# Latent attention on one core: the value products of two key blocks issued as one group

## The chip, the cores and the metric

The kernel runs on one core of a Trainium2 chip. The metric is the time on the device of one execution, in microseconds. The engines are TensorE (PE in the profile; PEld is its loading of weights), VectorE (DVE), ScalarE (ACT), GpSimd (POOL) and SyncE (SP), which issues most of the DMAs.

## The reference

Two layers work on 1024 latent tokens and 256 context tokens of width 1024. Each layer has a mixer of three head groups (retention, latent attention, windowed attention), an output projection, and a mixture of 16 experts. The change touches the latent attention, whose core is, for each of 8 heads:

```python
s = (einsum('bhqr,bkr->bhqk', ql, kv) + einsum('bhqp,bkp->bhqk', qr, kr)) * scale
p = softmax(s, axis=-1)
ol = einsum('bhqk,bkr->bhqr', p, kv)
out = einsum('blhr,rhd->blhd', ol, w_uv)
```

Latent tokens attend to all 1280 keys (context and latent). Context tokens attend to the 256 context keys, and in the first layer only.

## The kernel before, in words

Each layer runs in this order: adaptive norm and input projection with retention and windowed attention beside it (`front`), latent attention (`mla`), output projection (`out_proj`), experts (`moe`). All of this is one program; a scheduler puts the instructions of each engine in an order of its own from their priorities and from when it expects their inputs, within the limits of the data and the buffers.

In `mla` the keys and queries of a head are made in split form (a high and a low part), and the products run transposed: keys on the partitions, queries along the columns. The 1280 keys are 10 blocks of 128 (`NB`), the 1024 latent queries two halves `u` of 512. `main` (line 1125) handles one head. For each key block `kb` and each half `u`:

- `scores` (line 1083) makes three matmuls of 512 columns into a PSUM bank `st`, of which there are three.
- ScalarE takes the exponential into `P[kb][:, u]` (line 1142). `P` has four buffers, each for one key block with both halves.
- GpSimd adds `P[kb]` to `acc` (lines 1146 and 1148), the column sums before they are reduced over the partitions.
- `values` (line 1131) makes the products of the block's values with P. The output of half `u` goes to partitions 64u to 64u+63 of the one bank `po`, so that one product takes 64 of the 128 columns of the array. Each of these float32 products shows as two matmul instructions. All blocks accumulate into `po`.

In the loop `values(kb - 1)` is called in the turn of block `kb`, and `values(NB - 1)` after the loop. Its products have top priority (`high_priority`), and their order among themselves on TensorE is fixed (`manual_schedule`). Between these steps `advance` takes steps of three generators that run beside: `prep(h + 1)`, which makes the keys and queries of the next head and their row maxima (`top`, line 971: a product into one of the banks `sm`, of which there are three, or `sx`, of which there is one, and a maximum by VectorE, line 974); `finish` of the head before (line 1090: the copy of `po`, the products of `acc` with a column of ones, the reciprocals, the scaling); and in layer 0 `context` (line 1110), the attention of the context tokens. The last head has no next one to prepare. Its call `before_last` opens what the output projection and the routing need.

The scheduler, and not the text of the loop, thus sets where a group of value products stands among the score and preparation products. The text gives it the groups, their order inside, and the block whose exponentials a group needs.

Of the kernel before, what the change touches and what calls it, by code (L numbers as in the profile page):

```python
# [23 lines left out]
NB = 10  # L24
# [90 lines left out]
def hybrid_kernel(tc, I, out, dbg=None):  # L115
# [4 lines left out]
    def T(pool, shape, dt, tag, bufs=None):  # L120
        cnt[0] += 1
        kw = {} if bufs is None else {"bufs": bufs}
        return pool.tile(list(shape), dt, tag=tag, name=f"{tag}_{cnt[0]}", **kw)

    def mm(o, a, b, start, stop):
        PE.matmul(o, a, b, start=start, stop=stop, skip_group_check=True)  # L126
# [135 lines left out]
    def advance(gen, n=1):  # L262
        for _ in range(n):
            if next(gen, "end") == "end":
                return False
        return True
# [675 lines left out]
    def mla(l, M, qp, mp):  # L942
# [140 lines left out]
        def scores(o, h, ks, qs):  # L1083
            qh, ql = qTs[h % 2]
            kh, kl = M["kTs"][h % 2]
            mm(o, kh[:, ks], qh[:, qs], True, False)
            mm(o, kh[0:96, ks], ql[:, qs], False, False)
            mm(o, kl[:, ks], qh[0:96, qs], False, True)

        def finish(h, po, acc, n, c0):  # L1090


            c = "" if n == 512 else "c"
            ys = T(rp, [128, n], F32, "ys" + c, 1)
            acopy(ys[:, 0:n], po[:, 0:n])
            yield
            ps = bank()
            for u in range(2):
                mm(ps[64 * u:64 * u + 64, 0:n], ones, acc[:, u, 0:n], True, True)
            rb = T(rp, [128, n], F32, "rb" + c, 1)  # L1100
            r0 = 64 * (h % 2)
            acopy(rb[:, 0:n], ps[:, 0:n])
            for a in range(0, n, 128):
                V.reciprocal(rb[:, a:a + 128], rb[:, a:a + 128])
                yield
            for u in range(2):
                V.tensor_tensor(yT[r0:r0 + 64, h // 2, c0 + u * n:c0 + (u + 1) * n], ys[64 * u:64 * u + 64, 0:n],
                                rb[64 * u:64 * u + 64, 0:n], OP.mult)

        def context(h):  # L1110
            st = T(pp, [128, 512], F32, "st", 3)
            for kb in range(2):
                scores(st[:, kb * 256:kb * 256 + 256], h, slice(kb * 128, kb * 128 + 128), slice(0, 256))
            pc = T(rp, [128, 2, 2, 128], F32, "pc", 1)
            S.activation(pc.rearrange("p k u t -> p (k u t)"), st, AF.Exp, scale=scale)
            acc = T(rp, [128, 2, 128], F32, "accc", 1)
            G.tensor_tensor(acc, pc[:, 0], pc[:, 1], OP.add)
            yield
            po = bank()
            for kb in range(2):  # L1120
                for u in range(2):
                    mm(po[64 * u:64 * u + 64, 0:128], M["vn"][:, kb, h * 64:(h + 1) * 64], pc[:, kb, u], kb == 0, kb == 1)
            yield from finish(h, po, acc, 128, 0)

        def main(h, nxt, prev):

            acc = T(rp, [128, 2, 512], F32, "acc")
            po = T(pp, [128, 512], F32, "po", 1)
            P = {}

            def values(kb):
                with tc.high_priority(), tc.manual_schedule(engines={mybir.EngineType.PE}):
                    for u in (1, 0):
                        mm(po[64 * u:64 * u + 64], M["vn"][:, kb, h * 64:(h + 1) * 64], P[kb][:, u], kb == 0, kb == NB - 1)

            cx = context(h) if qb0 == 0 else None
            for kb in range(NB):
                P[kb] = T(rp, [128, 2, 512], F32, "P", 4)
                for u in range(2):
                    st = T(pp, [128, 512], F32, "st", 3)  # L1140
                    scores(st, h, slice(kb * 128, kb * 128 + 128), slice(CTX + u * 512, CTX + u * 512 + 512))
                    S.activation(P[kb][:, u], st, AF.Exp, scale=scale)  # L1142
                    if nxt is not None:
                        advance(nxt)
                if kb == 1:
                    G.tensor_tensor(acc, P[0], P[1], OP.add)
                elif kb > 1:
                    G.tensor_tensor(acc, acc, P[kb], OP.add)  # L1148
                if nxt is not None:
                    advance(nxt)  # L1150
                if kb > 0:
                    values(kb - 1)
                if nxt is not None:
                    advance(nxt)
                if prev is not None and kb >= 5:
                    advance(prev)
                if cx is not None and kb >= 3:
                    advance(cx)
            values(NB - 1)
            end = finish(h, po, acc, 512, CTX)  # L1160
            advance(end)
            while nxt is not None and advance(nxt):
                pass
            return end

        def run(yT_, rp_, pp_, before_last):
            nonlocal yT, rp, pp
            yT, rp, pp = yT_, rp_, pp_

            for tag, shape, bufs in (("pc", [128, 2, 2, 128], 1), ("accc", [128, 2, 128], 1), ("P", [128, 2, 512], 4),  # L1170
                                     ("acc", [128, 2, 512], 2)):
                T(rp, shape, F32, tag, bufs)
            prev = None
            for h in range(8):
                if h == 7:
                    before_last()
                prev = main(h, prep(h + 1) if h < 7 else None, prev)
            while advance(prev):
                pass
# [800 lines left out]
```

## Time and profile before

| | us |
|---|---|
| median of 3 runs | 2990.1 |
| lowest and highest | 2983.69, 2990.77 |
| the profiled execution | 2985.17 |
| its span in the profile | 2983.0 |
| PE busy | 2750.1 (92%) |
| DVE busy | 2166.1 (73%) |
| ACT busy | 1574.6 (53%) |
| POOL busy | 698.7 (23%) |
| value products (`po<-P,vn`), PE busy | 183.8 in 640 matmuls |

Latent attention runs from about 490 to 812 us (layer 0) and from about 2050 to 2357 us (layer 1). In a timeline the first number is the start of a piece and the second its length. Matmuls are pipelined, so that one starts before the end shown of the one ahead; what each costs is read from start to start.

### The profile page before, as it was taken

To read this page: it belongs to the slowest core of one execution; us is meant where nothing else is said; L and a number is where in the kernel's file an instruction comes from. 1 tells how busy PE (TensorE), PEld (TensorE's weight loads), DVE (VectorE), ACT (ScalarE), POOL (GpSimd) and SP (SyncE) were. 2 spreads that over 40 slices of the span, in tenths; PEclk is the share of its full clock that TensorE was granted. 3 is DMA by queue.
4 is the path that set the end of the run, shared out by engine and by line. 5 is a ranking of instruction groups with operands and counts; after the bars stand their busy time and mean duration, and the time that the engine had idled before them with its cause. 6 is when DMAs were issued, how large, how long until landed. Compare 5 with 4: busy or idle time off the path is not lost. (4 is left out here: it accounts for less than half of the span.)

```text
span 2983.0 us, 41643 instructions
## 1 busy us (share of the span) xinstructions
PE 2750.1 (92%) x14702; PEld 1885.9 (63%) x14702; DVE 2166.1 (73%) x4688; ACT 1574.6 (53%) x2728; POOL 698.7 (23%) x561
## 2 busy tenths in 40 slices
PE   7999998999999799999998799998999995999996
PEld 3666775556466566666665666785555573777774
DVE  4455668788748777777775755567878578899997
ACT  3353545555533456665664544346555434777774
POOL 0011133555611111111111010133555521111110
PEclk8999998999999899999999899899999997999998
DMA  8621210000278578887886422210000247999995
GB/s 302 232 79 57 85 38 7 1 1 1 85 263 284 182 261 285 278 287 256 282 275 211 154 87 66 85 44 1 1 1 23 79 174 268 342 372 392 387 383 198
DMA packets 177740, 507.93 MB, mean 170 GB/s; under 512 B 27110, under 2 KB 38172, under 8 KB 172412
## 3 DMA queue, kind: packets, MB, share of 16 engines
q1 hardware_dynamic: 158796, 443.40, 41.5%
q0 software_dynamic: 13552, 43.00, 5.7%
q10 hardware_dynamic: 5184, 18.88, 1.6%
q8 instruction: 116, 1.90, 0.3%
q14 instruction: 92, 0.75, 0.1%
HBM read 448.74 MB, written 56.46 MB: 169 GB/s over the span
## 5 line engine op out<-in xcount | busy, mean ns | idle before, releaser
L136 DVE TENSOR_TENSOR wlo<-raw,whi 128x1536 fp32r<-128x1536 f32 (+3 forms) x496 | 688.9, 1406 | 148.0 <-ACT whi L130 144.9
L130 ACT ACTIVATE whi<-raw 128x1536 fp32r<-128x1536 f32 (+3 forms) x496 | 591.1, 1207 | 271.4 <-DMA raw<-in_exp_w_up_dram 89.9
L1148 POOL TENSOR_TENSOR acc<-acc,P 128x1024 f32<-128x1024 f32 x128 | 306.8, 2397 | 180.7 <-ACT P L1142 178.6
L126 PE MATMUL pp<-whi,hhs 128*128 128x512 f32 (+3 forms) x640 | 255.1, 400 | 4.4 <-DVE st L288 2.7
L1142 ACT ACTIVATE P<-st 128x512 f32<-128x512 f32 x320 | 187.3, 594 | 119.5 <-PE st L126 115.4
L126 PE MATMUL pp<-wlo,hhs 128*128 128x512 f32 (+3 forms) x640 | 248.6, 389 | 0.2 <-DVE wlo L136 0.2
L126 PE MATMUL pp<-whi,hl 128*128 128x512 f32 (+3 forms) x640 | 247.4, 387 | 0.8 <-DVE hl L136 0.7
L126 PE MATMUL pg<-whi,xh 128*128 128x512 f32 x720 | 224.7, 419 | 1.8 <-ACT xh L130 1.8
L126 PE MATMUL pg<-wlo,xh 128*128 128x512 f32 x720 | 213.3, 401 | 0.4 <-DVE wlo L136 0.3
L126 PE MATMUL pg<-whi,xl 128*128 128x512 f32 x720 | 210.0, 397 | 0.0
L1813 POOL DMA_INDIRECT xres<-ys,idx x31 | 82.4, 2658 | 523.0 <-DVE ys L1812 523.0
L974 DVE TENSOR_REDUCE mx<-sm 128x1 f32<-128x512 f32 (+1 forms) x308 | 172.2, 585 | 34.6 <-PE sm L126 31.1
L126 PE MATMUL po<-P,vn 128*64 128x512 f32 x640 | 183.8, 627 | 10.6 <-ACT P L1142 8.9
L126 PEld LDWEIGHTS pg<-whi,xh 128*128 128x128 f32 x720 | 128.9, 191 | 44.1 <-issue 19.8
L126 PEld LDWEIGHTS pg<-whi,xl 128*128 128x128 f32 x720 | 137.1, 191 | 29.5
L126 PEld LDWEIGHTS pg<-wlo,xh 128*128 128x128 f32 x720 | 136.0, 191 | 31.1 <-DVE wlo L136 1.8
L126 PEld LDWEIGHTS pp<-whi,hhs 128*128 128x128 f32 x640 | 125.1, 196 | 31.5 <-issue 5.1
L126 PEld LDWEIGHTS pp<-wlo,hhs 128*128 128x128 f32 x640 | 125.0, 195 | 24.4 <-issue 8.0
L126 PEld LDWEIGHTS pp<-whi,hl 128*128 128x128 f32 x640 | 125.2, 196 | 22.6 <-issue 3.8
L126 PE MATMUL st<-qTl,kTh 96*128 96x512 f32 (+1 forms) x336 | 137.7, 410 | 0.0
L126 PE MATMUL st<-qTh,kTh 97*128 97x512 f32 (+1 forms) x336 | 135.8, 404 | 1.9 <-ACT vn L130 1.3
L126 PE MATMUL st<-qTh,kTl 96*128 96x512 f32 (+1 forms) x336 | 132.8, 395 | 0.0
(502 smaller groups left out, 5581.5 us busy)
## 6 DMA issues: line engine op xcount, KB each, us to landing
raw<-in_exp_w_gate_dram SPq DMA_DIRECT2D x256, 384.0 KB
raw<-in_exp_w_up_dram SPq DMA_DIRECT2D x256, 384.0 KB
raw<-in_exp_w_down_dram SPq DMA_DIRECT2D x192, 512.0 KB
w<-in_ada_w_dram SPq DMA_DIRECT2D x40, 1024.0 KB
projd<-st SPq DMA_DIRECT2D x54, 256.0 KB
raw<-in_w_in_dram SPq DMA_DIRECT2D x48, 256.0 KB
hl<-in_ada_w_dram SPq DMA_DIRECT2D x16, 512.0 KB
xt<-in_x_dram SPq DMA_DIRECT2D x16, 512.0 KB
```

What stands on the lines that cost most here:

```text
L126: PE.matmul(o, a, b, start=start, stop=stop, skip_group_check=True)
L130: S.activation(o, i, AF.Copy)
L136: V.tensor_sub(lo, src, hi)
L974: V.tensor_reduce(mx[:, b, j:j + 1], o[:, 0:z - a], AX.X, OP.max)
L1142: S.activation(P[kb][:, u], st, AF.Exp, scale=scale)
L1148: G.tensor_tensor(acc, acc, P[kb], OP.add)
L1813: G.indirect_dma_start(out=xres[l], out_offset=bass.IndirectOffsetOnAxis(ap=idx[:, :1], axis=0), in_=ys, in_offset=None, compute_op=OP.add)
```

## The change

`values` makes the products of two key blocks, the newer one (`kb`) first and then the older (`kb - 1`), each with half 1 ahead of half 0. It is called in the turns of blocks 2, 4, 6 and 8, for the pairs (1, 0), (3, 2), (5, 4) and (7, 6), and after the loop for (9, 8). The accumulation therefore starts with block 1 and ends with block 8. Priority and the fixed order now cover the four products of a pair.

```diff
             def values(kb):
+
                 with tc.high_priority(), tc.manual_schedule(engines={mybir.EngineType.PE}):
-                    for u in (1, 0):
-                        mm(po[64 * u:64 * u + 64], M["vn"][:, kb, h * 64:(h + 1) * 64], P[kb][:, u], kb == 0, kb == NB - 1)
+                    for k in (kb, kb - 1):
+                        for u in (1, 0):
+                            mm(po[64 * u:64 * u + 64], M["vn"][:, k, h * 64:(h + 1) * 64], P[k][:, u], k == 1, k == NB - 2)
...
-                if kb > 0:
+                if kb > 0 and kb % 2 == 0:
                     values(kb - 1)
```

## Rows read from the trace of the kernel before

**Rows 1.** The page, busy time of each engine.

```profile
PE 2750.1 (92%) x14702; PEld 1885.9 (63%) x14702; DVE 2166.1 (73%) x4688; ACT 1574.6 (53%) x2728; POOL 698.7 (23%) x561
```

**Rows 2.** By stretch: length; PE, PEld, DVE, ACT, POOL busy; clock, DMA share, GB/s.

```profile
633.90:675.00 41.10, 39.85 (x182) 24.25 (x178) 35.07 (x62) 23.19 (x47) 22.02 (x11) 1.00 0.00 0
...
2112.00:2151.40 39.40, 37.81 (x159) 21.28 (x158) 31.56 (x57) 21.19 (x42) 21.47 (x9) 1.00 0.00 1
...
1200.00:1400.00 200.00, 193.09 (x1282) 131.83 (x1284) 154.00 (x169) 123.07 (x139) 34.66 (x18) 0.98 0.83 279
2540.00:2700.00 160.00, 160.00 (x751) 125.96 (x750) 151.02 (x165) 119.92 (x130) 20.40 (x11) 1.00 0.99 362
```

**Rows 3.** Timeline of TensorE, layer 0: one value group and its neighbours.

```profile
599.78 0.40 PE L126 MATMUL st<-qTl,kTh 96*128 96x512 f32 x1
600.11 1.08 PE L126 MATMUL po<-P,vn 128*64 128x512 f32 x4
601.12 0.49 PE L126 MATMUL st<-qTh,kTl 96*128 96x512 f32 x1
601.46 0.28 PE L126 MATMUL sx<-kTh,qTh 96*128 96x256 f32 x1
601.57 0.39 PE L126 MATMUL st<-qTh,kTh 97*128 97x512 f32 x1
...
602.04 0.40 PE L126 MATMUL st<-qTh,kTl 96*128 96x512 f32 x1
```

**Rows 4.** Value products of tile po; minimum, median, maximum in ns.

```profile
L126 PE MATMUL po<-P,vn x640: 592/593/1117, 490.8 to 2354.5; 128*64 128x512 f32 x160
```

**Rows 5.** Timeline of TensorE, start of the last head of layer 0.

```profile
781.39 2.06 PE L126 MATMUL po<-P,vn 128*64 128x512 f32 x8 [0.79 <-ACT ys L130]
783.37 0.50 PE L126 MATMUL st<-qTh,kTh 97*128 97x512 f32 x1
783.72 0.40 PE L126 MATMUL st<-qTl,kTh 96*128 96x512 f32 x1
```

**Rows 6.** Timeline of TensorE, layer 1, end of a head.

```profile
2108.13 0.64 PE L126 MATMUL po<-P,vn 128*64 128x512 f32 x1
2108.20 0.59 PE L126 MATMUL sm<-acc,mcst 128*64 128x512 f32 x1
```

**Rows 7.** Waits, layer 0, 590 to 757 us: total, times, longest.

```profile
PEld po L126 <- ACT P L1142: 12.7, 32, 0.7
...
PE po L126 <- ACT P L1142: 2.3, 8, 0.3
```

**Rows 8.** Waits, layer 1, 2110 to 2308 us.

```profile
PE po L126 <- ACT P L1142: 1.3, 3, 0.5
```

**Rows 9.** Waits, layer 0, 590 to 757 us, with VectorE in them.

```profile
DVE mx L974 <- PE sm L126: 7.5, 16, 1.2
...
DVE rb L1104 <- ACT rb L130: 4.8, 4, 1.2
DVE mx L974 <- PE sx L126: 4.8, 6, 1.2
...
DVE qTl L1019 <- ACT qTh L130: 4.6, 4, 1.1
...
PE sm L126 <- DVE mx L974: 2.4, 4, 0.6
```

**Rows 10.** By line, 592 to 757 us: busy, mean ns, idle before.

```profile
L1148 POOL TENSOR_TENSOR acc<-acc,P 128x1024 f32<-128x1024 f32 x33 | 78.3, 2372 | 47.3 <-ACT P L1142 47.3
...
L974 DVE TENSOR_REDUCE mx<-sm 128x1 f32<-128x512 f32 (+1 forms) x77 | 42.2, 575 | 7.2 <-PE sm L126 6.9
```

**Rows 11.** Timeline of TensorE, layer 1, the last head.

```profile
2346.39 1.08 PE L126 MATMUL po<-P,vn 128*64 128x512 f32 x4
...
2351.59 1.08 PE L126 MATMUL po<-P,vn 128*64 128x512 f32 x4
...
2356.68 1.98 PE L126 MATMUL sm<-acc,mcst 128*64 128x512 f32 x4 [1.58 <-POOL acc L1148]
```

## The prediction

> **What bounds the kernel now.** I read the page's busy shares first. TensorE is busy for 2750.1 of 2983.0 us, VectorE for 2166.1, ScalarE for 1574.6 [rows 1]. An average hides stages, so the second view is busy time by stretch. The change touches latent attention alone: eight heads in each of two layers. One head of layer 0 takes 41.1 us, in which TensorE is busy 39.85, VectorE 35.07, ScalarE 23.19, GpSimd 22.02 and DMA moves nothing; a head of layer 1 takes 39.4 us with TensorE at 37.81 [rows 2]. [...] The experts' stage that follows is again TensorE's (193.09 of 200 us, and 160.00 of 160 us in layer 1) [rows 2]. It starts when attention has ended, so what a head gives back should move everything behind it forward.
>
> The third view is the order of TensorE's instructions. Score products of 512 columns follow each other every 0.235 us (601.57 and, two on, 602.04) [rows 3]. The value products of one key block are four instructions of 64 columns, two at a time on the two halves of the array, together 1.01 us (600.11 to 601.12) [rows 3]. What the reader is to see is what stands around them: the matmul ahead has its successor 0.33 us after its start (599.78 to 600.11) where 0.235 is usual, and the first one behind needs 0.34 (601.12 to 601.46). About 0.1 us is thus lost on each side of a group.
>
> **What the change does, and the cost of each part.** Nothing is computed less: 640 value instructions stay, 4 for a block, so 160 blocks [rows 4]. The calls go from ten of one block to five of two blocks, for each head.
>
> *Merging two groups.* A group now costs 1.01 us and the two edges, 0.095 and 0.105: 1.21 us, two of them 2.42. The trace holds one place where two blocks ran back to back, at the start of the last head of layer 0: eight instructions from 781.39 to 783.37, 1.98 us, with 0.35 to the second score product behind [rows 5]. With the same edges that is 2.18 us. A merged pair saves 0.24 us. Two blocks of a head already share their edges with other 64-column work, for instance the block that runs among the products of the sums with a column of ones at 2108 us [rows 6]; I count those as saving nothing, and pair the other eight. 4 pairs x 16 heads x 0.24 = 15.4 us off the path. From below this term is 0 (pairs that do not form), from above 80 pairs x 0.24 = 19 us.
>
> [...]
>
> *Waiting for the exponentials.* A group at top priority is put on TensorE as soon as its exponentials are expected. TensorE's idle time for them is 2.3 us in 8 waits over four heads of layer 0 and 1.3 us in 3 waits over five heads of layer 1 [rows 7, 8], 0.58 and 0.26 us a head. With the newer block first a merged group waits once, for the later exponential, and the older block is long there. Half as many groups wait: 0.29 x 7 + 0.13 x 7 = 2.9 us gained. The weight-load rows put up to 12.7 us over four heads on the same releaser [rows 7], 3.2 us a head, but most of that is the 0.25 us edge already counted. From above, then, half of what is left, some 0.5 us a head, 7 us; from below, a loss: each of 64 groups may wait 0.2 us more, 13 us. I take 2.9, since that row is idle time of TensorE itself.
>
> *What stands behind a longer group.* For 2.0 instead of 1.0 us TensorE issues nothing else. Queued behind are score products, for which ScalarE waits, and products of the next head's preparation, for which VectorE waits. ScalarE has 18 us free in a head [rows 2] and three score banks. VectorE has 6.0 us free in layer 0; of these 7.5 + 4.8 us over four heads, 3.1 a head, are waits for TensorE's preparation banks [rows 9]. TensorE in turn waits 2.4 us over four heads, 0.6 a head, for VectorE to empty a bank [rows 9]. I let that grow by half, 0.3 us in each of the 14 heads that prepare another: 4.2 us lost. Bounds: 0, and the 20 us of the first rival.
>
> *Buffers of P.* The older block of a pair is held one block longer, with four buffers: two are held, two stay for blocks ahead. GpSimd's sum takes 2.37 us a block and was waiting for P before most of these [rows 10]. So it holds no buffer longer than TensorE does; cost nothing. If GpSimd did fall behind, the exponentials would come late next.
>
> *The end of a layer.* The last head has no preparation beside it. There a block takes 2.6 us (2346.39 and, two blocks on, 2351.59) and the last group is followed by a wait of 1.58 us for GpSimd's sum [rows 11]. GpSimd's 2.37 us is close to the 2.5 us that a block would take, and the last two sums come closer together. I take back half of the gain of both last heads: 1.0 us.
>
> *The single bank po.* The first products of a head need it free from the copy of the head before. Today they come with block 0, then with block 1, so the copy has more time: cost nothing.
>
> Sum: 15.4 + 2.9 - 4.2 - 1.0 = 13.1 us. The profiled execution took 2985.17 us (span 2983.0 and 2.2 around it); less 13.1 that is 2972. It lies 5 us below the median of the runs, 2990.1; the mean of these three and of the profiled one is 2987.4, from which the forecast is 2974.
>
> **The rivals.**
>
> 1. *Slower: VectorE starves during the long groups.* VectorE lives on what TensorE puts into four banks; a bank holds 0.58 us of its work on average [rows 10]. If its backlog at a group's start is 0.9 us, an old group of 1.2 us leaves it idle 0.3 us, ten times a head: 3 us, which is the 3.1 us seen. A merged one of 2.2 us leaves 1.3 us, five times: 6.5. With 35.1 us of work and 2.35 us of its other waits (4.8 + 4.6 over four heads [rows 9]) a head of layer 0 would then take 44.0 us, 2.9 more; over seven heads 20 us slower than 2987, about 3007. It decides if the backlog is below some 1.5 us, at which VectorE's total meets TensorE's new pace. Against it: all four banks full are 2.3 us, TensorE can fill a bank in 0.235 us, and preparation is due only at the head's end. [...] Chance 0.10.
>
> 2. *No change: the saved edges turn into waits.* The newer exponential is waited for with nothing of the older block left to run in the meantime. Today the older group could fill that time. At 0.2 us for each of 64 groups this is 12.8 us in place of the 2.9 gained; 15.4 - 12.8 - 4.2 - 1.0 is -2.6, so 2990. For it: waits of 0.3 us stand before present groups. Against it: score and preparation products fill today's gaps too. Chance 0.14.
>
> 3. *The change does not do what it says.* Order is fixed among the four products only; other matmuls may be put between the two blocks, as the column-of-ones products are today [rows 6]. If half the pairs are split, half of every term is left, 6.5 us: 2981. Chance 0.08.
>
> 4. *More than forecast.* If half of the upper wait bound comes too and VectorE costs nothing, 19 + 7 = 26 us, about 2961. Chance 0.08.
>
> **How the numbers follow.** The forecast has 0.60, and its own range is a gain of 9 to 20 us, 2967 to 2979. About 0.3% (9 us) is what a measurement of this kernel can tell from no change. Forecast and rival 4 lie beyond it: faster 0.68. Rivals 2 and 3 lie within it: same 0.22. Rival 1: slower 0.10. The range runs from rival 4, 2960, to 2991, past rivals 2 and 3 but short of the first, which leaves out some 0.15 to 0.2.
>
> **What would show it.** In the changed trace the value products should stand as runs of eight of about 1.98 us, some 64 to 80 of them, with an edge of 0.1 us at each end. Heads should take 40.3 and 38.6 us. TensorE's idle time for P should fall by about half. VectorE's waits for TensorE's banks may rise by 1 to 2 us a head without a longer head; if they rise and the head does not shorten, rival 1 is right. If TensorE's waits for P grow in place of the edges, it is rival 2; if runs of four remain, rival 3. The forecast is wrong if a head shortens by less than 0.5 us, or if a gain in the heads is lost again in the output projection or the experts.

## The result, and the profile after

The changed kernel takes 3029.3 us (median of 4 runs, 3027.0 to 3035.1) against 2989.3 us for the kernel before on the same chip: a ratio of 1.0136 with a 95% interval of 1.0118 to 1.0155. It is 40 us slower, where the sum had forecast 13 us less (2974). The profiled execution took 3030.5 us.

The page of the changed kernel, its busy times, to be held against [rows 1]:

```profile
span 3028.6 us, 41576 instructions
...
PE 2755.3 (91%) x14702; PEld 1904.1 (63%) x14702; DVE 2198.3 (73%) x4688; ACT 1571.3 (52%) x2728; POOL 703.4 (23%) x561
```

By this page every engine runs exactly as many instructions as before. TensorE's busy time has grown by 5 us only, though its groups are shorter. VectorE's has grown by 32 us with the same 4688 instructions, and that is the first thing to ask about.

The time is lost in latent attention. From the first value product to the last, layer 0 now takes 344.9 us instead of 317.0, layer 1 314.4 instead of 303.8: 38.5 of the 45.6 us by which the span grew. By stretch, two heads of layer 0, one of layer 1, and three stretches inside the first of them (columns as in [rows 2]):

```profile
610.22:657.67 47.45, 42.58 (x179) 25.88 (x178) 39.07 (x62) 22.89 (x48) 22.19 (x11) 0.93 0.00 1
657.67:705.37 47.70, 43.51 (x179) 26.90 (x178) 39.27 (x62) 22.92 (x48) 22.22 (x11) 0.89 0.00 0
2194.70:2236.70 42.00, 37.44 (x158) 22.56 (x157) 33.44 (x57) 20.66 (x42) 21.72 (x10) 0.96 0.00 1
610.22:632.00 21.78, 19.81 (x87) 11.76 (x86) 20.30 (x26) 11.19 (x23) 9.72 (x5) 1.00 0.00 0
632.00:639.20 7.20, 4.30 (x16) 2.63 (x15) 6.88 (x12) 4.12 (x9) 2.52 (x2) 0.90 0.00 0
639.20:643.20 4.00, 4.00 (x11) 0.94 (x10) 2.04 (x4) 0.14 (x1) 2.36 (x1) 0.50 0.00 0
```

The head of layer 0 shown in [rows 2] took 41.10 us, with 35.07 of VectorE in 62 instructions at a granted clock of 1.00. These take 47.5, with 39.1 us of VectorE in the same 62, and the clock is 0.93 and 0.89. Inside the first head it is 1.00 up to 632.0. In the next 7.2 us TensorE is busy for 4.3 only, while VectorE has hardly a gap, and the mean clock is 0.90: for the last 1.4 us of this stretch, from about 637.8 on, it is at 0.50, and it stays there in the stretch behind.

The groups themselves came out as meant. The value products of the changed kernel:

```profile
L126 PE MATMUL po<-P,vn x640: 592/592/1117, 492.2 to 2398.1; 128*64 128x512 f32 x160
```

They stand in 74 runs of eight; the other pairs, one in each of six heads, are split by products of the column sums. At a granted clock of 1.00 a run of eight takes 1.87 us to the start of its successor (627.94 to 629.81 in the timeline below). So what has to be explained is not the merged group.

### What VectorE does longer

Timelines of the changed kernel over the same 30 us of the first of these heads: VectorE, GpSimd, ScalarE and TensorE (start, length, instruction, idle time before it and what ended it). GpSimd's instructions here are its sums of P, the `acc` of line 1148 (the first of a head) and 1150.

```profile
618.42 3.52 DVE L1107 TENSOR_TENSOR yB<-ys,rb 64x512 f32<-64x512 f32 x2
...
628.08 2.79 DVE L1029 TENSOR_TENSOR qTl<-tb,qTh 32x512 fp32r<-32x512 f32 x1
...
632.34 0.68 DVE L1024 TENSOR_TENSOR tb<-tb,ta 32x512 f32<-32x512 f32 x1
...
633.96 0.68 DVE L1029 TENSOR_TENSOR qTl<-tb,qTh 32x512 fp32r<-32x512 f32 x1
...
636.03 1.82 DVE L1024 TENSOR_TENSOR tb<-tb,ta 32x256 f32<-32x256 f32 x1
```

```profile
615.88 4.82 POOL L1150 TENSOR_TENSOR acc<-acc,P 128x1024 f32<-128x1024 f32 x2 [2.96 <-ACT P L1144]
627.97 2.36 POOL L1148 TENSOR_TENSOR acc<-P,P 128x1024 f32<-128x1024 f32 x1 [7.27 <-ACT P L1144]
635.20 2.38 POOL L1150 TENSOR_TENSOR acc<-acc,P 128x1024 f32<-128x1024 f32 x1 [4.87 <-ACT P L1144]
```

```profile
621.98 0.60 ACT L130 ACTIVATE ys<-po 128x512 f32<-128x512 f32 x1 [1.05 <-DVE yB L1107]
...
633.06 0.63 ACT L130 ACTIVATE qTh<-tb 32x512 fp32r<-32x512 f32 x1 [2.33 <-DVE tb L1024]
633.71 0.60 ACT L1144 ACTIVATE P<-st 128x512 f32<-128x512 f32 x1
```

```profile
627.94 1.94 PE L126 MATMUL po<-P,vn 128*64 128x512 f32 x8 [0.88 <-ACT P L1144]
629.81 0.50 PE L126 MATMUL sm<-hhs,wqs 128*128 128x256 f32 x2
...
632.45 0.36 PE L126 MATMUL sx<-kTh,qTh 96*128 96x256 f32 x1 [0.38 <-DVE tb L1023]
...
634.36 0.50 PE L126 MATMUL st<-qTh,kTh 97*128 97x512 f32 x1 [0.74 <-ACT P L1144]
...
635.70 0.92 PE L126 MATMUL sm<-kTh,qTh 96*128 96x512 f32 x2 [0.60 <-DVE tb L1023]
...
638.36 0.79 PE L126 MATMUL sm<-kTh,qTh 96*128 96x512 f32 x1 [1.17 <-DVE mx L974]
...
639.51 3.68 PE L126 MATMUL po<-P,vn 128*64 128x512 f32 x8
643.12 0.80 PE L126 MATMUL sm<-kTh,qTh 96*128 96x512 f32 x1
```

Read it in order of time. The same instruction `qTl<-tb,qTh`, of the same shape, takes 0.68 us at 633.96 and 2.79 us at 628.08. At 628.08 GpSimd has just begun a sum, which ends at 630.33; the instruction ends at 630.87, 0.54 us later. What VectorE has behind it moves back by 2.1 us, among it `tb` at 632.34. ScalarE waits 2.33 us for that `tb`, and the exponential that stands behind it in ScalarE's order begins only at 633.71. TensorE runs out of score banks (0.74 us at 634.36). The next `tb`, at 636.03, meets the next sum: it takes 1.82 us, where the shortest of its shape takes 0.42, and ends 0.27 us after the sum. TensorE waits 1.17 us for the maximum that VectorE makes behind it (638.36). Within this wait its granted clock falls from 1.00 to 0.50, and a run of eight takes 3.61 us (639.51 to 643.12) instead of 1.87.

The pattern holds for four kinds of VectorE instruction whose two operands and output all lie in SBUF: `tb<-tb,ta` (line 1024 before and after), `qTl<-tb,qTh` (1029), and both forms of `yB` (1107), 132 in all. Reductions, reciprocals and operations with one operand in a PSUM bank keep their length beside GpSimd's sums. In the kernel before, beside a sum and without one, the maxima of 512 columns out of `sm` (line 974) take 673 to 693 and 664 to 693 ns, the reciprocals `rb<-rb` (1104) 891 to 953 and 894 to 954, and `tb<-sm,tabs` of 512 columns (1023), with one operand in a bank, 689 to 690 and 689. I call **excess** the sum, over these 132, of duration less the shortest of the same shape in the same run. It is 61.9 us before and 98.9 us after, in 50 and 61 instructions that are over 0.2 us too long. The tiles of the kernel before:

```profile
L1029 DVE TENSOR_TENSOR qTl<-tb,qTh x42: 417/550/1931, 493.9 to 2296.3; 32x512 fp32r<-32x512 f32 x21, 32x256 fp32r<-32x256 f32 x21
```

```profile
L1107 DVE TENSOR_TENSOR yB<-ys,rb x32: 683/944/2899, 568.2 to 2363.5; 64x512 f32<-64x512 f32 x32
```

and of the changed kernel:

```profile
L1029 DVE TENSOR_TENSOR qTl<-tb,qTh x42: 416/682/2794, 493.0 to 2344.6; 32x512 fp32r<-32x512 f32 x21, 32x256 fp32r<-32x256 f32 x21
```

```profile
L1107 DVE TENSOR_TENSOR yB<-ys,rb x32: 682/2232/2901, 571.2 to 2406.8; 64x512 f32<-64x512 f32 x32
```

Where no sum runs beside them, six `yB<-ys,rb` of the kernel before and ten of the changed one take 684 to 692 ns. This tile has one shape, and a maximum of four times the minimum was there to be read before the change already; after it even the median is three times the minimum. `qTl` has two shapes, whose shortest take 0.42 and 0.68 us; its maximum of 1.93 us before and 2.79 after lies far above both.

Who waits for these instructions stands in the waits of the whole run (total, times, longest). Before:

```profile
ACT qTh L130 <- DVE tb L1024: 35.3, 29, 2.8
...
PE sm L126 <- DVE mx L974: 9.3, 19, 0.6
PE po L126 <- ACT P L1142: 8.9, 19, 2.5
ACT ys L130 <- DVE yB L1107: 8.0, 7, 3.2
```

After:

```profile
ACT qTh L130 <- DVE tb L1024: 65.4, 33, 3.1
ACT ys L130 <- DVE yB L1107: 31.8, 13, 4.5
PE sm L126 <- DVE mx L974: 20.4, 23, 1.7
PE st L126 <- ACT qTh L130: 11.7, 6, 2.2
PE sm L126 <- DVE tb L1023: 8.1, 12, 1.7
PE po L126 <- ACT P L1144: 7.2, 12, 1.1
```

Two channels run from VectorE to TensorE. One is the query rotation of the next head: `tb` late, ScalarE's copy `qTh` late (35.3 to 65.4 us), and the exponentials behind it. The other is the end of the head before: `yB` reads the one buffer `ys`, ScalarE's copy of `po` into `ys` must wait for it (8.0 to 31.8 us), and again exponentials and `qTh` copies stand behind. TensorE's direct wait for P did not grow (8.9 to 7.2 us).

### The profile page after: what moved, and what is told of

Same layout as the page of the kernel before. It is cut to its first block, busy times and chain, and to the rows that moved or that the text cites. A ratio compares the mean times of both kernels' runs of the same rounds, so it can differ in the third digit from the quotient of the medians.

```text
span 3028.6 us, 41576 instructions
## 1 busy us (share of the span) xinstructions
PE 2755.3 (91%) x14702; PEld 1904.1 (63%) x14702; DVE 2198.3 (73%) x4688; ACT 1571.3 (52%) x2728; POOL 703.4 (23%) x561
## 5 line engine op out<-in xcount | busy, mean ns | idle before, releaser
L126 PE MATMUL po<-P,vn 128*64 128x512 f32 x640 | 174.4, 656 | 7.4 <-ACT P L1144 7.2
L126 PE MATMUL sm<-kTh,qTh 96*128 96x512 f32 (+1 forms) x308 | 113.1, 405 | 34.7 <-DVE mx L974 20.2
```

## The experiments

The theory, A in the texts on record: GpSimd's sum of P keeps VectorE's operations with both operands in SBUF standing; pairs shift the order so that more of them meet a sum, and the rest follows through the two channels. The other letters stand for its rivals: B is that the long groups themselves leave VectorE and ScalarE without work; C that the harm is done in the first half of a head, where the next head is prepared; D that the sums hold the buffers of P too long. All ratios are to the kernel before, with 95% intervals.

### GpSimd's sums cut

In both kernels the sum was cut to 16 of the 512 columns of each half, and the first one of a head was replaced by a constant. The column sums are therefore left out for the most part; TensorE, VectorE and ScalarE have the same instructions.

```diff
                 if kb == 1:
-                    G.tensor_tensor(acc, P[0], P[1], OP.add)
+                    G.memset(acc, 1.0)
                 elif kb > 1:
-                    G.tensor_tensor(acc, acc, P[kb], OP.add)
+                    G.tensor_tensor(acc[:, :, 0:16], acc[:, :, 0:16], P[kb][:, :, 0:16], OP.add)
```

With pairs:

> The changed kernel with GpSimd's sums of P cut to 16 of 512 columns of each half (the rest of the column sums is left out, so the output is not the reference's); the order of TensorE, VectorE and ScalarE is the changed kernel's. Theory A (VectorE's additions between two SBUF operands stand still while GpSimd adds, 2.8 us where 0.68 is usual, and with sums two in a row this makes the long groups late): about 2985 us or less, that is 40 us or more below the changed kernel, and level with or below the light form of the kernel before. Theory B (TensorE's 1.9 us groups leave VectorE and ScalarE without work, whatever GpSimd does): 3015 to 3030 us, and 30 us or more above the light form of the kernel before.

With single blocks:

> The kernel before with the same cut of GpSimd's sums, as the control. Theory A: a gain of 5 to 15 us over the kernel before, since VectorE's additions wait for GpSimd there too (yB 3.59 us for two), smaller than the gain of the changed kernel by 30 us or more. Theory B: within 5 us of the kernel before.

Measured: 2924.4 us with pairs (0.9799, 0.9777 to 0.9821), 2943.9 with single blocks (0.9872, 0.9838 to 0.9906). The excess falls to 1.0 and 0.8 us. With pairs that is what A expected and far from B. With single blocks the gain of 41 us is more than the 5 to 15 that A expected: the sums cost the kernel before far more than was thought. The two tiles with pairs:

```profile
L1029 DVE TENSOR_TENSOR qTl<-tb,qTh x42: 416/550/684, 493.0 to 2248.5; 32x512 fp32r<-32x512 f32 x21, 32x256 fp32r<-32x256 f32 x21
```

```profile
L1107 DVE TENSOR_TENSOR yB<-ys,rb x32: 682/686/781, 558.8 to 2304.6; 64x512 f32<-64x512 f32 x32
```

The maximum of `yB` is 781 ns instead of 2901. And without the sums pairs are 19.5 us faster than single blocks, some 11 us either way by the spread of the runs: the whole loss of 40 us, and the missing gain, hang on GpSimd's sums. Long groups alone cost nothing. This does not yet say by which way the sums do it.

### Which pairs

Pairs in the late half of the head alone, (5, 4), (7, 6), (9, 8), with blocks 0 to 3 single; then pairs in the early half alone, (1, 0) and (3, 2). The groups by the turn in which they are called (abridged: in the kernels the table stands in the line itself, and `values` takes the blocks that it is given):

```diff
-                if kb > 0:
-                    values(kb - 1)
+                for ks in GROUPS.get(kb, ()) and (GROUPS[kb],):
+                    values(*ks)
...
+late:  GROUPS = {1: (0,), 2: (1,), 3: (2,), 4: (3,), 6: (5, 4), 8: (7, 6)}, and (9, 8) after the loop
+early: GROUPS = {2: (1, 0), 4: (3, 2), 5: (4,), 6: (5,), 7: (6,), 8: (7,), 9: (8,)}, and (9,) after the loop
```

> Blocks 0 to 3 alone, as before; pairs (5, 4), (7, 6) and (9, 8). Theory A and theory C (the harm is done while the next head's keys and queries are made, in the first four blocks of a head, where a merged group waits for the later exponential and preparation stands behind it): 2970 to 2985 us, a gain of some 0.2 us a merge, 10 us in all. Theory B: about three fifths of the loss, 3010 us.

> Pairs (1, 0) and (3, 2); blocks 4 to 9 alone. Theories A and C: nearly the whole loss, 3015 to 3030 us. Theory B: about two fifths of it, 3005 us.

Measured: late pairs 2994.8 us (1.0031, 1.0007 to 1.0055), early pairs 3008.0 (1.0089, 1.0057 to 1.012). Both expectations of A were missed. Late pairs should have gained, and early pairs should have cost nearly the whole; they cost 23 us, about what B had said (3005). Neither half is free, which speaks against C; between A and B these two times do not decide. The excess is 81.7 and 71.1 us. ScalarE's waits tell the two apart. Late pairs:

```profile
ACT qTh L130 <- DVE tb L1024: 33.9, 22, 2.8
ACT ys L130 <- DVE yB L1107: 31.9, 13, 4.5
```

Early pairs:

```profile
ACT qTh L130 <- DVE tb L1024: 60.7, 35, 3.1
...
ACT ys L130 <- DVE yB L1107: 7.0, 6, 3.2
```

Each half opens one channel and leaves the other as it was in the kernel before (35.3 and 8.0). Late pairs delay `yB`, early pairs the query rotation, and the changed kernel has both.

### Is it the engine at work, or the buffer held?

Two kernels with pairs. In the first GpSimd lets P go early: it reads 16 columns of each half and then multiplies `acc` by itself over all 1024 (the column sums are left out). In the second each sum is made in two halves of 512, P being held as long as before.

```diff
                 if kb == 1:
-                    G.tensor_tensor(acc, P[0], P[1], OP.add)
-                elif kb > 1:
-                    G.tensor_tensor(acc, acc, P[kb], OP.add)
+                    G.memset(acc, 1.0)
+                if kb > 0:
+                    G.tensor_scalar(acc[:, :, 0:16], P[kb][:, :, 0:16], 0.0, 1.0, OP.mult, OP.add)
+                    G.tensor_tensor(acc, acc, acc, OP.mult)
```

> The changed kernel in which GpSimd takes only 16 columns of each half of P and then multiplies acc (all ones) by itself over the full 1024 columns (the column sums of P are left out, so the output is not the reference's). GpSimd is as busy between its SBUF operands as with the sums, but lets go of P at once; the other engines keep the changed kernel's order. Theory A (VectorE's two-operand SBUF work stands still while GpSimd's runs): it stays slow, 3020 to 3040 us, with some 90 to 100 us of excess in VectorE's additions. Rival D (GpSimd holds the four buffers of P too long once blocks come in pairs, so that exponentials come late): fast, 2925 to 2945 us, as with the cut sums.

The first sum of a head is halved in the same way (left out here):

```diff
...
                 elif kb > 1:
-                    G.tensor_tensor(acc, acc, P[kb], OP.add)
+                    for u in range(2):
+                        G.tensor_tensor(acc[:, u], acc[:, u], P[kb][:, u], OP.add)
```

> The changed kernel with each of GpSimd's sums made in two halves of 512 columns. Theory A: a VectorE addition can wait at most for the half that runs, if it gets in between two halves: excess about half of 98.9 us, time 2995 to 3010 us. If VectorE gets in only when GpSimd pauses: no change, 3020 to 3035 us. Rival D: P is let go no earlier, so no change.

Measured for the first: 2967.2 us (0.9931, 0.9908 to 0.9955), excess 39.0. It fell between the two expectations. The operation put in is not as long as the sum:

```profile
L1151 POOL TENSOR_TENSOR acc<-acc x144: 1892/1895/2312, 493.1 to 2323.8; 128x1024 f32<-128x1024 f32 x144
```

1.9 us, not the 2.37 of [rows 10], and whether that accounts for the lower excess is not shown. So by itself it decides nothing.

Measured for the second: 2971.4 us (0.995, 0.9925 to 0.9975), 58 us below the changed kernel and below the 2995 to 3010 that A expected; excess 51.5. (All 16 `yB` of the context tokens are held up here, the shortest for 0.45 us; against the 0.27 us that the shortest takes before, the excess is 58.7.) The work is the same, no buffer is released sooner, and the sum takes 2 x 1.28 us, a little more than in one piece. Only the time for which one GpSimd instruction runs has become shorter. One collision, on VectorE and on GpSimd:

```profile
616.80 1.70 DVE L1029 TENSOR_TENSOR qTl<-tb,qTh 32x512 fp32r<-32x512 f32 x1
```

```profile
616.69 1.27 POOL L1149 TENSOR_TENSOR acc<-P,P 128x512 f32<-128x512 f32 x1 [0.20 <-ACT P L1144]
```

The instruction stands until 617.96, the end of the half sum, and is done 0.54 us later: 1.0 us lost, where the whole sum had cost it 2.1. That speaks against D, which had no reason to expect a gain here. So do ScalarE's waits for a buffer of P that a sum still holds. In the kernel before they are

```profile
ACT P L1142 <- POOL acc L1148: 0.2, 1, 0.2
```

and the changed kernel has none. The same edit with single blocks came with the next set.

### The scaling moved to GpSimd: a miss

If VectorE stands still in `yB` for GpSimd's sake, GpSimd could do `yB` itself, and the two would never meet there. With pairs and with single blocks:

```diff
-                V.tensor_tensor(yT[...
+                G.tensor_tensor(yT[...
```

> The changed kernel with the last product of a head (yB, ys times rb) moved from VectorE to GpSimd. It is 57 of the 98.9 us of excess and some 2 us of VectorE's work a head besides. Theory A: 2975 to 2995 us. Theory B (the long group itself): within 10 us of the changed kernel, 3020 to 3035 us. Rival D: slower than the changed kernel, since GpSimd has more to do ahead of its sums.

> The kernel before with the same move, as the control. Theory A: 35 us of its 61.9 us of excess go, of which some were hidden: a gain of 10 to 25 us, 2962 to 2977 us; the changed kernel with the move should then lie within 15 us of it. Theory B and rival D: within 5 us of the kernel before, or slower.

Measured: 3045.0 us (1.0183, 1.0156 to 1.0211) with pairs, 3001.2 (1.0039, 1.0016 to 1.0062) with single blocks; both slower, against the expectation of A. The excess of the 84 operations that stay on VectorE is 36.8 and 27.3 us (41.5 and 26.9 without the move), and that of `yB` is gone. The waits with pairs:

```profile
ACT ys L130 <- POOL yB L1107: 67.2, 13, 8.0
...
PE st L126 <- ACT qTh L130: 46.5, 12, 7.6
```

`yB` now stands behind GpSimd's sums in GpSimd's own order and comes later still, so ScalarE's copy `ys` waits up to 8.0 us at a time. So VectorE's excess is not the price by itself: what waits for `yB`, this copy with all that ScalarE has behind it, sets it. D had forecast a slower kernel here, but ScalarE has no wait for a buffer of P held by a sum in this run either. The run sets the second channel apart from the first.

### The second channel closed

The steps that finish the head before are begun one turn earlier, so that `yB` is done sooner:

```diff
-                if prev is not None and kb >= 5:
+                if prev is not None and kb >= 4:
```

With late pairs, with single blocks, then the halved sums with single blocks, and halved sums and earlier finish with all pairs:

> Blocks 0 to 3 alone, the rest in pairs, and the head before is finished one block earlier (its generator is advanced from block 4 instead of 5, so that yB comes with block 8). Theory A1 (with late pairs the two last sums of a head run while yB is due; yB stands still, the next head's copy of po into the one ys buffer waits for it on ScalarE, and the exponentials queue behind that copy): ScalarE's waits for yB fall from 31.9 us to under 10, and the time from 2995 to 2970 to 2980 us. If the late pairs cost time by themselves, it stays at 2990 to 3000.

> The kernel before with the same earlier finish, as the control. Theory A1: little to win (8.0 us of such waits): 2978 to 2990 us, and 5 to 10 us above the late pairs with the same finish.

> The kernel before with GpSimd's sums in two halves, the control for the changed kernel with halves (2971 us). Theory A: about half of 61.9 us of excess goes, of which some 0.7 were on the path: 2962 to 2975 us, so that with halves pairs and single blocks lie within 10 us of each other. If halves helped only where blocks come in pairs: 2980 to 2990 us.

> The changed kernel with sums in halves and the earlier finish. If both channels add: 2950 to 2965 us, ahead of the kernel before and of each of the two edits alone. If the halves have already removed the wait for yB (6.2 us are left): 2965 to 2975 us.

| kernel | us | ratio, interval | excess |
|---|---|---|---|
| late pairs, earlier finish | 2986.2 | 0.9994, 0.9976 to 1.0012 | 64.6 |
| single, earlier finish | 2977.6 | 0.9973, 0.9958 to 0.9989 | 60.1 |
| single, halved sums | 2969.8 | 0.9933, 0.9909 to 0.9957 | 49.1 |
| pairs, halved sums, earlier finish | 2961.8 | 0.992, 0.989 to 0.995 | 54.2 |

The excess is that of the profiled execution, which took 2987.1 us for the third row and so lies at the upper end of its runs. In the fourth row the shortest `yB` of the context is again one that was held up; against 0.27 us the excess is 57.4.

ScalarE's waits with late pairs and the earlier finish:

```profile
ACT qTh L130 <- DVE tb L1024: 34.9, 27, 2.8
...
ACT ys L130 <- DVE yB L1107: 2.2, 1, 2.2
```

The wait for `yB` is gone (31.9 to 2.2 us) and 8.6 us with it; that is less than was expected (2970 to 2980). Late pairs still lie 8.7 us above single blocks with the same edit. A good part of the excess stands in the context tokens' `yB` (25.3 of the 64.6 us; 19.3 with late pairs alone, 7.0 in the kernel before); whether that is the rest, no run here settles.

### The first channel closed at VectorE

Here GpSimd's sums stay whole. The rotation of the query is kept in the PSUM bank `o` that it comes from, so that both operations of the first channel have one operand there (for every head but the first of a layer, whose branch is left out here):

```diff
...
                 V.tensor_tensor(ta[64:96, 0:n], o[96:128, 0:n], M["tabs"][96:128, a:z], OP.mult)
-                V.tensor_tensor(tb[64:96, 0:n], o[64:96, 0:n], M["tabs"][64:96, a:z], OP.mult)
-                V.tensor_tensor(tb[64:96, 0:n], tb[64:96, 0:n], ta[64:96, 0:n], OP.add)
+                V.tensor_tensor(o[64:96, 0:n], o[64:96, 0:n], M["tabs"][64:96, a:z], OP.mult)
+                V.tensor_tensor(o[64:96, 0:n], o[64:96, 0:n], ta[64:96, 0:n], OP.add)
+                turning[a] = o
```

> Pairs (1, 0) and (3, 2), the rest alone, and the rotation of the next head's queries kept in its PSUM bank, so that the addition tb and the difference qTl of VectorE have one operand outside SBUF; GpSimd's sums are whole. Theory A: the excess of tb and qTl goes from 40 us to about 0, ScalarE's waits for tb from 60.7 to under 30 us, and the time from 3008 to 2980 to 2990 us. If the early pairs cost time for a reason other than these two operations: 3000 to 3015 us. If the bank, held longer, is missed elsewhere: slower.

> The kernel before with the same rotation, as the control. Theory A: 27 us of excess go, most of them hidden (its waits for tb were 35.3 us): 2970 to 2983 us; the early pairs with the same edit should come within 10 us of it, where they were 23 us apart.

> The changed kernel with sums in halves, the earlier finish and the rotation in PSUM. Theory A: only yB is left to collide, some 30 us of excess: 2945 to 2958 us, the fastest whole kernel of the study. If the longer hold of the bank takes it back: 2960 to 2970.

> The kernel before with sums in halves and the earlier finish, the control for the changed kernel with both (2962 us). Theory A: with collisions mostly gone a pair saves its edges, 10 us over the stage, so this one should take 2965 to 2975 us. If pairs save nothing: 2955 to 2962 us.

> Single blocks with halves, earlier finish and the rotation in PSUM: the control for the fastest kernel (2934 us). If pairs save their edges once few collisions are left: 2943 to 2952 us, 10 to 18 us above it. If pairs save nothing: 2928 to 2940 us.

> The changed kernel with the earlier finish and the rotation in PSUM, GpSimd's sums whole: each of the two channels closed at VectorE, none at GpSimd. If the two channels are the whole of the loss: 2945 to 2965 us, 65 us or more below the changed kernel. If whole sums, two in a row, do harm in yet another way: 2975 us or more.

| kernel | us | ratio, interval |
|---|---|---|
| early pairs, rotation in PSUM | 2956.1 | 0.9891, 0.9874 to 0.9908 |
| single, rotation in PSUM | 2959.5 | 0.9912, 0.9893 to 0.993 |
| pairs, rotation in PSUM, earlier finish | 2954.8 | 0.9888, 0.9869 to 0.9907 |
| single, halved sums, earlier finish | 2960.7 | 0.9916, 0.9899 to 0.9933 |
| single, halved sums, rotation in PSUM, earlier finish | 2946.5 | 0.9862, 0.983 to 0.9894 |
| pairs, halved sums, rotation in PSUM, earlier finish | 2933.9 | 0.9817, 0.9793 to 0.984 |

The early pairs alone are the sharp case: 3008.0 us become 2956.1, with nothing changed on GpSimd or in the groups. ScalarE's waits for the rotation fall from 60.7 to 20.4 us. The 52 us are more than A expected (2980 to 2990) and more than the 40 us of excess that the two operations had; where the rest comes from is not shown. The operation that had waited, with its operand in a bank:

```profile
L1035 DVE TENSOR_TENSOR qTl<-sm,qTh x28: 422/422/689, 493.2 to 2271.8; 32x256 fp32r<-32x256 f32 x16, 32x512 fp32r<-32x512 f32 x12
```

Its maximum is 689 ns; with both operands in SBUF it had been 2800 in the same arrangement. The third row closes both channels on VectorE's side: all pairs and whole sums take 2954.8 us, 74.6 less than the changed kernel. The last row is the fastest of all. Its attention stages, columns as in [rows 2]:

```profile
556.00:740.00 184.00, 180.68 (x838) 112.39 (x837) 157.61 (x293) 111.67 (x225) 114.31 (x90) 1.00 0.03 10
2070.00:2260.00 190.00, 189.07 (x823) 112.04 (x822) 154.67 (x295) 109.35 (x215) 122.05 (x96) 1.00 0.04 10
```

TensorE is busy 98.2% and 99.5% of the time at a granted clock of 1.00. The control with halved sums and the earlier finish came out where pairs save nothing (2955 to 2962 expected for that case), against A's 2965 to 2975. What pairs bring can now be set out by how much of the standing still is left:

| the rest of the kernel | single | pairs | difference |
|---|---|---|---|
| as it was | 2989.3 | 3029.3 | +40.0 |
| halved sums | 2969.8 | 2971.4 | +1.6 |
| halved sums, earlier finish | 2960.7 | 2961.8 | +1.1 |
| the same, rotation in PSUM | 2946.5 | 2933.9 | -12.6 |
| sums cut | 2943.9 | 2924.4 | -19.5 |

The single and paired kernels of rows 2 to 4 ran on different chips; their intervals against the kernel before overlap in rows 2 and 3, and by 0.001 in row 4. Only the first and last rows, each measured side by side, separate without doubt.

## Why the prediction was wrong

- *Merging two groups.* Right in kind, and by the rows too small. Runs of eight came out 74 times, at 1.87 us where 1.98 was expected from the one place that showed it. Two groups of 1.01 less 1.87 is 0.15 us, and with one pair of edges, 0.20, a merged pair saves 0.35 us, not 0.24: as an estimate 26 us over 74 runs. With the sums cut pairs give 19.5 us, 0.26 each; the spread of those runs leaves room for 0.24 and 0.35 alike. The sum's first two terms together were 15.4 + 2.9.
- *Waiting for the exponentials.* Right in direction: TensorE's wait for P fell from 8.9 to 7.2 us over the run, by less than the 2.9 us of the sum. (The edge of 0.25 us in the upper bound of this term stands in none of its rows; the edges read there were 0.1.)
- *What stands behind a longer group.* This is the step that failed. It took VectorE's 35.07 us a head as fixed and let only its waits for banks pass on to TensorE, 4.2 us in all. But those 35.07 us held stalls: by the mean of each group less its shortest instruction, 3.9 us in that head (2.2 in two `yB`, 1.6 in three `tb`, 0.2 in two `yB` of the context). After the change it is 8.2 us (2.1 in two `yB`, 2.6 in three `yB` of the context, 2.1 in two `qTl`, 1.4 in a `tb`), and VectorE's busy time 39.1: the 4 us more are stall. That takes 4 of the 6.0 us which were counted as free, and the late instructions stand in the way of ScalarE and TensorE: the term of 4.2 us for two layers stands against 6.4 us in this one head. Stall inside an instruction does not show as a wait in any row of [rows 9]; it shows as spread between minimum and maximum of a tile.
- *The single bank po.* Wrong as well. The bank has more time, but the copy out of it writes `ys`, of which there is one, and that waits for `yB`: 31.8 us instead of 8.0, with the exponentials queued behind. The step looked at one end of the copy only.
- *Buffers of P.* Held up: the changed kernel has no wait of ScalarE for a buffer that a sum holds, and halving the sums without releasing P sooner gave back 58 us.
- *The end of a layer* was not separated by a run.
- *The first rival* named the right engine and sign with another mechanism. VectorE is not starved by long groups (with the sums cut they cost nothing); it is stopped by GpSimd. Its price of 20 us was half of the loss. The sign that it had named for itself came true all the same: VectorE's waits for TensorE's preparation banks rose from 43.6 to 61.0 us over the run, about 1.2 us a head, and the heads grew longer.
- *The amplifier.* No term allowed for the clock. After several idle pieces of TensorE of 0.4 to 1.2 us (632 to 638 us) the granted clock is 0.50, and the next group costs 1.7 us more (3.61 for 1.87); that the idle pieces bring the clock down is the author's reading, which no run tests by itself. In the head of 47.45 us, 2.7 us of the 6.3 added are TensorE's busy time and 3.6 its idle time.

What the prediction lacked is that the length of these VectorE instructions depends on what GpSimd does beside them. The traces show how: all of the 50 and 61 instructions held up start while a sum runs and end 0.55, 0.28 or 0.15 us after it, by their 512, 256 or 128 columns. Undisturbed they take 0.68, 0.42 and 0.27 us, 0.13 us more at each width, so the part that grows with the columns was all still to be done. The other order shows as well: a sum that begins when such an instruction has 0.47 us to go takes 2.67 to 2.72 us instead of 2.38. With one operand in a bank the longest `qTl` falls from 2800 to 689 ns. This spoke against the change: a shift in the order of these engines redrew who meets whom (50 held up before, 61 after).

**What stays open.** Why pairs meet the sums more often and for longer than single blocks (61 times and 1.6 us each against 50 and 1.2) is shown in part. With pairs the sums come two in a row (4.82 us at 615.88): of 144 sums 39 follow the one before within 0.1 us, where 4 did. That belongs to the late pairs, which alone have 35; the early pairs have 9. In the query rotation the number of collisions is nearly the same (29 before, 30 after), but seven `qTl` of 512 columns now meet a head's first sum near its start and lose 1.9 us each, where one met a sum before. Why the scheduler's order falls so is not shown. As an estimate, an instruction put down at random would find GpSimd at a sum with 22.0/41.1 = 0.54 chance and lose 1.2 us on average (half of a sum's 2.37), 85 us for 132: the order before lay below chance, that after above it. Nor is the excess a price by itself: with halved sums and the earlier finish pairs have 57.4 us of it (against 0.27 us for the shortest `yB` of the context) and single blocks 34.4, at the same time. What decides is who queues behind. More buffers for P or for `ys`, and the older block first, were not run.

## What to carry to other kernels

Before pricing a change that only reorders, look at minimum, median and maximum of equal-shaped instructions of the engine next to the bound: a wide spread can be stall that hides as work (here `yB`, 683 to 2899 ns), and reordering can redraw it (here the excess went from 61.9 to 98.9 us). Where GpSimd makes long sums (here 2.37 us) beside VectorE, give VectorE's operations on the path one operand in PSUM, or cut GpSimd's instruction into shorter ones; here these gave 27 and 16 us on the kernel before, and the merged groups 19.5 with the sums cut. For every copy, price both ends: the buffer that it frees and the buffer that it must wait for.

## What the runs showed of the hardware

- Halving GpSimd's sum costs almost nothing: 2 x 1.28 us against 2.38 for the whole, and each collision loses about half (0.8 us on average against 1.6), though 72 of the 132 are held up where 61 were.
- The size of the clock's part: a run of eight value products takes 1.87 us at a granted clock of 1.00 and 3.61 us at 0.50. Idle pieces of TensorE of 0.38, 0.74 and 0.60 us between 632.1 and 635.7 us, and the first half of one of 1.17, came before the clock fell at about 637.8.
